# A hybrid encoder layer on one core: attention steps handed out ahead of the norm and rotation pieces

## The chip, the core and the metric

The kernel runs on one core of a Trainium2 chip, in one launch. The metric is the device time in microseconds. Five engines work side by side, each through its own queue in program order: TensorE (PE in the profile, with its weight loads as PEld), VectorE (DVE), ScalarE (ACT), GpSimd (POOL) and SyncE (SP), which issues most transfers. An instruction that waits holds everything behind it on its own engine.

## The reference

One layer over 512 tokens of width 1024, in float32. Three token mixers run in parallel, are gated and merged, and an expert-choice mixture of experts follows:

```python
z = x @ w_in                       # NA q|k|v, GQA q|k|v, memory q, gates
y_na  = neighbourhood_attention(q_na, k_na, v_na, rpb)     # 8 heads of 64
# gqa_attention, 8 query heads and 2 key heads of 64:
q = apply_rope(rms_norm(q, q_gain), cos, sin)
k = apply_rope(rms_norm(k, k_gain), cos, sin)
y_gqa = softmax(q @ k.T / sqrt(64)) @ v
y_mem = softmax(q_m @ mk.T / sqrt(128)) @ mv               # 4 heads of 128, 256 memory tokens
merged = sum_g sigmoid(gate_g(x)) * (y_g @ w_branch[g])
x = LN(alpha * x + merged @ w_out)
x = LN(alpha * x + ExpertChoiceMoE(x))                     # 16 experts, SwiGLU, capacity 64
```

The change touches the part in which the rotated, normalised queries and keys of the second mixer (GQA) are made, and the order in which the attention of the first two mixers to run (memory, then GQA) is handed out beside it.

## The kernel before, in words

The order of work on every engine is written out by hand: the program text is the order. A dense product is kept exact enough by splitting both factors into a high and a low part and adding three products; the weights stream in as 74 units of 128 x 1024 (`Stream`, transfers issued on SyncE, split on ScalarE (high, L87) and VectorE (low, L88)).

The stages are generators. Each `yield` in one of them ends a *round*: the products of this round have been issued on TensorE, and their evacuation from PSUM follows when the generator goes on. `run(gen, every, delay)` walks through the rounds and puts two sorts of work into each:

- a *piece* from the list `bg`, at most one for each round;
- an *attention step* (`at.step`), when the count `acc`, which grows by `every` in each round, has reached 1.

A step advances a pipeline over three attention units at once: the scores S of a new unit, the transposes T of the unit before, the product PV of the one before that, all on TensorE; then `soft` (maximum on VectorE, exponential on ScalarE), `tev` (evacuation of the transposes), `norm` (scaling by the reciprocal sum on VectorE, L536) and `yev`. T of a unit, one step later, reads what `norm` wrote. The scores have two PSUM banks (tag "S"), the transposes two ("T"), PV one ("Y"), and all dense products and the rotation transposes share three ("mm").

The pieces of GQA's rotary part come from `rope_stages`, one list for each group of heads: group 0 is the keys, groups 1 and 2 are four query heads each. A list is: s1 the square (ACT, L360); s2 the sum of squares and a reciprocal root in small VectorE instructions (L363 to L96); s3 two multiplications (VectorE, L368, L369); s4 the rotation, six instructions on POOL (L379 to L382); then transposes on TensorE with copies on ScalarE and subtractions on VectorE: `sk` for the keys (rT at L388, kk at L396 and L398), `sq_(0)` and `sq_(1)` for the two head pairs of a query group (rT at L388, qs at L408 and L409). Below, a0 to a5 are the six pieces of group 1 and b0 to b5 those of group 2, counted as in the diff (a[4] is a4); so a3 and b3 are the rotations, and a4, a5, b4, b5 the transposes. All groups share one scratch for squares and rotation.

`g_gqa` has twelve rounds, four for each group ("projection rounds" 1 to 12), each of 24 products of 256 columns. Its memory-attention steps come at `every` = 0.85. A group's list is added to `bg` behind its fourth round. Then `g_branch(2)` runs ("branch rounds" 1 to 16): two gate products of 24 matmuls of 512 columns each, then two projections of 12, four times over. GQA's steps begin in branch round 4 and come in every round. After it follow the value rounds of the neighbourhood attention (`g_na_v`) with the rest of the steps.

Before the change the pieces fall on these rounds: keys s1 to s4 on projection rounds 5 to 8, `sk` on 9; a0 to a2 on 10 to 12; a3 on branch round 1, a4 on 2, a5 on 3; b0 to b5 on 4 to 9; then `norm_hi`, `norm_mask` and `norm_lo`, which prepare rows of the layer norms, on 10 to 12. In each round the piece stands ahead of the step.

Later stages use `run` too: `g_na_gates` has a short list of router pieces beside steps of the neighbourhood attention. The expert stage at the end streams its weights through a ring of lent buffers: when TensorE has used up the block in a buffer, the transfer of the next block into it is issued.

Of the kernel before, what the change touches and what calls it, by code (L numbers as in the profile page):

```python
# [59 lines left out]
def layer_kernel(ctx: ExitStack, tc: tile.TileContext, xt, xn, first0, wu, bgate, rpb, gains, wrt,  # L60
# [14 lines left out]
    def R(tag, shape, name, dt=F32, bufs=None):  # L75
        return rp.tile(shape, dt, name=name, tag=tag, bufs=bufs)
# [3 lines left out]
    def PB(tag, name, shape=(P, 512)):  # L80
        return ps.tile(list(shape), F32, name=name, tag=tag, bufs=PS_BUFS[tag])

    def small(shape, name, dt=F32, bufs=2):
        return sp.tile(shape, dt, name=name, tag=name, bufs=bufs)
# [5 lines left out]
    def rsqrt(y, v, hv, a):  # L90
        nc.vector.tensor_scalar(y.bitcast(I32), v.bitcast(I32), -0.5, RSQRT_SEED, op0=ALU.mult, op1=ALU.add)
        nc.vector.tensor_scalar(hv, v, -0.5, None, op0=ALU.mult)
        for _ in range(3):
            nc.vector.tensor_tensor(a, y, y, op=ALU.mult)
            nc.vector.tensor_tensor(a, a, hv, op=ALU.mult)
            nc.vector.scalar_tensor_tensor(y, a, 1.5, y, op0=ALU.add, op1=ALU.mult)  # L96
# [181 lines left out]
    def n_chunk(acc, us, ah, al, m, hooks={}):  # L278
        c = slice(m * P, (m + 1) * P)
        for k in range(KD):  # L280
            hooks.get(k, lambda: None)()
            h = us[k // 4][0].rearrange("p (k c) -> p k c", k=4)[:, k % 4]
            lo = us[k // 4][1].rearrange("p (k c) -> p k c", k=4)[:, k % 4]
            nc.tensor.matmul(acc, ah[:, k, c], h, start=(k == 0), stop=False)
            nc.tensor.matmul(acc, ah[:, k, c], lo, start=False, stop=False)
            nc.tensor.matmul(acc, al[:, k, c], h, start=False, stop=(k == KD - 1))
# [60 lines left out]
    bg = []  # L347

    def rope_stages(q, zs, nh, which):
        n = NT * nh  # L350
        z = zs.rearrange("p m (h f) -> p (m h) f", f=64)
        sqf, t = ST["rope"]
        sq = sqf[:, :n * 64].rearrange("p (g f) -> p g f", f=64)
        t = t[:, :n * 64]
        zr = ST["zr"][:, q % 2, :n * 64]
        ss = small([P, n], f"ss{n}", bufs=1)
        rs = small([P, n], f"rs{n}", bufs=1)

        def s1():
            nc.scalar.activation(sq, z, AF.Square)  # L360

        def s2():
            nc.vector.tensor_reduce(ss, sq, axis=AX.X, op=ALU.add)  # L363
            nc.vector.tensor_scalar(ss, ss, 1.0 / 64.0, RMS_EPS, op0=ALU.mult, op1=ALU.add)
            rsqrt(rs, ss, small([P, n], f"sh{n}", bufs=1), small([P, n], f"sa{n}", bufs=1))

        def s3():
            nc.vector.tensor_tensor(z, z, rs[:, :, None].to_broadcast([P, n, 64]), op=ALU.mult)  # L368
            nc.vector.tensor_tensor(z, z, gain_t[:, which, None, :].to_broadcast([P, n, 64]), op=ALU.mult)  # L369

        def s4():
            z2 = zs.rearrange("p m (h i two) -> p m h i two", i=32, two=2)
            u2 = sqf[:, :n * 64].rearrange("p (m h i two) -> p m h i two", m=NT, i=32, two=2)
            t2 = t.rearrange("p (m h i two) -> p m h i two", m=NT, i=32, two=2)
            d2 = zr.rearrange("p (m h i two) -> p m h i two", m=NT, i=32, two=2)
            cb = csn_t[:, :, 0, None, :].to_broadcast([P, NT, nh, 32])
            sb = csn_t[:, :, 1, None, :].to_broadcast([P, NT, nh, 32])
            for i in range(2):
                nc.gpsimd.tensor_tensor(t2[:, :, :, :, i], z2[:, :, :, :, i], cb, op=ALU.mult)  # L379
                nc.gpsimd.tensor_tensor(u2[:, :, :, :, i], z2[:, :, :, :, 1 - i], sb, op=ALU.mult)  # L380
            for i, op in enumerate((ALU.subtract, ALU.add)):
                nc.gpsimd.tensor_tensor(d2[:, :, :, :, i], t2[:, :, :, :, i], u2[:, :, :, :, i], op=op)  # L382

        def heads_T(pair):
            tp = PB("mm", f"rT{q}{pair}", (P, NT, P))
            zc = zr.rearrange("p (m c) -> p m c", m=NT)
            for m in range(NT):
                nc.tensor.transpose(tp[:, m], zc[:, m, pair * P:(pair + 1) * P], ident)  # L388
            return tp.rearrange("p m c -> p (m c)")

        def sk():
            tp = heads_T(0)
            for g in range(2):
                src = tp[g * 64:g * 64 + 64]
                for o in (0, 64):
                    nc.scalar.copy(khh[o:o + 64, g], src)  # L396
                for o in (0, 64):
                    nc.vector.tensor_tensor(klo[o:o + 64, g], src, khh[o:o + 64, g].bitcast(F32), op=ALU.subtract)  # L398

        def sq_(pair):  # L400
            hp = 2 * (q - 1) + pair
            tp = heads_T(pair)
            for h in range(2):
                src = tp[h * 64:h * 64 + 64]
                d = ST["qs"][hp // 2][:, 2 * (hp % 2) + h]
                hb = 64 * (hp // 2)
                lb = 64 - hb
                nc.scalar.copy(d[hb:hb + 64], src)  # L408
                nc.vector.tensor_tensor(d[lb:lb + 64], src, d[hb:hb + 64].bitcast(F32), op=ALU.subtract)  # L409

        khh, klo = ST["khh"], ST["klo"]
        if which:
            return [s1, s2, s3, s4, sk]
        return [s1, s2, s3, s4, lambda: sq_(0), lambda: sq_(1)]

    def g_gqa():
        kk = R("Q6", [P, 4, S], "kk", F32R)
        qs = R("Q4", [P, 8, S], "qs", F32R)
        ST["b01"] = b01 = R("Q5", [P, 4, 1024], "ropevg")
        b1t = b01[:, 2:4]  # L420
        vg = b1t[:, 0, :512].rearrange("p (m f) -> p m f", m=NT)
        ST.update(khh=kk[:, 0:2], klo=kk[:, 2:4], vg=vg, qs=(qs[:, 0:4], qs[:, 4:8]),
                  rope=(vs_t[:, 0], b1t[:, 1]), zr=b01[:, 0:2])
        for q in range(3):
            us = ws.take(2)
            zs = ST["A5" if q % 2 else "A6"][:, 1, :512 if q == 0 else 1024].rearrange("p (m c) -> p m c", m=NT)
            for m in range(NT):
                acc = PB("mm", f"gq{q}{m}")
                n_chunk(acc[:, :256], us, xh, xl, m)
                ws.prefetch(2 if m == NT - 1 else 1)  # L430
                yield
                if q == 0:
                    nc.scalar.copy(zs[:, m], acc[:, :P])
                    nc.scalar.copy(vg[:, m], acc[:, P:256])
                else:
                    nc.scalar.copy(zs[:, m], acc[:, :256])
            bg.extend(rope_stages(q, zs, 2 if q == 0 else 4, 1 if q == 0 else 0))

    def g_na_v():
        v = ST["b01"][:, 0:2].rearrange("p a (b f) -> p (a b) f", f=S)  # L440
# [28 lines left out]
    def g_branch(g, first, pre=None):  # L469
        if first:  # L470
            ST["macc"] = R("M", [P, KD, S], "macc")
        macc = ST["macc"]
        for jp in range(4):
            th = []
            for jj in range(2):
                t = R("t", [P, S], f"th{g}{jp}{jj}", bufs=2)
                th.append(t)
                ev = gate_piece(g, 2 * jp + jj, t)
                yield
                ev()  # L480
            u, = ws.take()
            ws.prefetch()
            for jj in range(2):
                j = 2 * jp + jj
                acc = proj_piece(u, jj, *ST[f"y{g}"], f"pr{g}{j}")
                yield
                if first:
                    nc.vector.scalar_tensor_tensor(macc[:, j], th[jj], 1.0, acc, op0=ALU.add, op1=ALU.mult)
                else:
                    tmp = R("tmp", [P, S], f"tm{g}{j}", bufs=2)  # L490
                    nc.vector.scalar_tensor_tensor(tmp, th[jj], 1.0, acc, op0=ALU.add, op1=ALU.mult)
                    nc.gpsimd.tensor_tensor(macc[:, j], macc[:, j], tmp, op=ALU.add)
            if pre:
                yield from pre(jp)
# [265 lines left out]
    def run(gen, every=0.0, delay=0):  # L760
        acc = -every * delay
        for _ in gen:
            if bg:
                bg.pop(0)()
            acc += every
            while acc >= 1.0:
                acc -= 1.0
                at.step()


    class Ring:
# [84 lines left out]
    yg = R("Q2", [P, 8, S], "yg", F32R)  # L856
    ST["y1"] = (yg[:, 0:4], yg[:, 4:8])
    at.add([GqaUnit(hp, m) for hp in range(4) for m in range(NT)])
    bg.extend([norm_hi, norm_mask, norm_lo])
    run(g_branch(2, True), 1.0, 3)  # L860
    run(g_na_v(), 1.0)
    at.drain()
# [866 lines left out]
```

## Time and profile before

| | |
|---|---|
| runs | 977.21, 979.08, 1060.49 us; median 979.08 |
| profiled execution | 977.92 us |
| its span in the profile | 976.1 us |
| granted TensorE clock, mean | 0.995 |
| TensorE busy | 944.4 us, 97% of the span |
| VectorE, ScalarE, GpSimd busy | 451.9, 274.3, 78.4 us |
| moved by DMA | 251.62 MB, 258 GB/s in the mean |

Busy time counts instructions of an engine, not its queue's waits. The span is measured from the first to the last instruction that the profile shows, and 1.8 us of the profiled execution lie outside it. The stage that the change touches runs from about 80 to 180 us. In the views used below, a row of the order of time is: start, length, engine, line, operation, output<-inputs, shape, count, and in brackets the idle time before it and what released it. A row of waits is: who waited for whom, us in total, times, the longest. Line numbers are those of the kernel before.

### The profile page before, as it was taken

Reading aid. Unit: us, or ns where it says so; the run is one execution under the profiler, and the core shown is the slowest. Engines: PE = TensorE matmul, PEld = TensorE weight load, DVE = VectorE, ACT = ScalarE, POOL = GpSimd, SP = SyncE. Lnnn points to the kernel's source line nnn. Section 1 sums busy time; section 2 is a strip of 40 time slices with the busy share of each in tenths; the row PEclk is TensorE's granted clock in tenths of the full one; section 3 lists DMA queues with packets and bytes.
Section 4 is the critical chain, followed back from the end, with each engine's and each line's share of the span. In section 5 each row is a group of like instructions: output and inputs, shape, how many; then the busy total and the mean of one; then the engine's idle time right before and its main releaser. Section 6 shows DMA issues by size and latency. Waiting matters only on the chain.

```text
span 976.1 us, 13068 instructions
## 1 busy us (share of the span) xinstructions
PE 944.4 (97%) x5350; PEld 615.0 (63%) x5350; DVE 451.9 (46%) x857; ACT 274.3 (28%) x540; POOL 78.4 (8%) x86
## 2 busy tenths in 40 slices
PE   8999899999999999999999999999999998997996
PEld 8899787889888888887886333433343332432344
DVE  6347678765376566237464155331332222231426
ACT  5343345444354454323223000100010000100123
POOL 0002403000032231000013000000000000000003
PEclk9999999999999999999999999999999999999998
DMA  9312121111333322584719999999999999999992
GB/s 357 111 68 65 65 65 44 65 44 58 85 117 111 101 82 75 217 325 183 279 50 389 389 422 430 430 433 429 429 430 430 430 430 431 432 429 431 428 419 100
DMA packets 38473, 251.62 MB, mean 258 GB/s; under 512 B 12543, under 2 KB 12927, under 8 KB 24590
## 3 DMA queue, kind: packets, MB, share of 16 engines
q1 hardware_dynamic: 37982, 249.74, 63.5%
q10 hardware_dynamic: 432, 1.05, 0.3%
q8 instruction: 42, 0.69, 0.3%
q14 instruction: 17, 0.14, 0.0%
HBM read 247.89 MB, written 2.10 MB: 256 GB/s over the span
## 4 chain that ended last, share of the span: by engine, by line
PE 70%; DMA 18%; DVE 6%; ACT 2%; POOL 2%; issue 1%; SPq 0%; DVEq 0%; POOLq 0%; ACTq 0%
DMA w<-in_wx 17%; PE g L1254 7%; PE u L1254 7%; PE y L1287 6%; PE gate L269 4%; PE gate L271 4%; PE gate L270 4%; PE nqk L271 1%; PE nqk L270 1%; PE nqk L269 1%; PE gy L627 1%; PE pr L269 1%; PE pr L270 1%; PE pr L271 1%; PE ga L1216 1%
## 5 line engine op out<-in xcount | busy, mean ns | idle before, releaser
L1254 PE MATMUL g<-w,xs 128*64 128x512 f32 x512 | 134.7, 604 | 7.5 <-DMA w<-in_wx 7.5
L1254 PE MATMUL u<-w,xs 128*64 128x512 f32 x512 | 131.6, 592 | 0.0
L1287 PE MATMUL y<-w,hT 128*64 128x512 f32 x480 | 107.0, 594 | 4.6 <-DMA w<-in_wx 3.9
L87 ACT CAST y<-y 64x512 fp32r<-64x512 f32 x30 | 17.4, 579 | 240.3 <-PE y L1287 229.0
L88 DVE TENSOR_TENSOR y<-y,y 64x512 fp32r<-64x512 f32 x30 | 20.7, 689 | 135.2 <-ACT y L87 135.2
L1254 PEld LDWEIGHTS u<-w,xs 128*64 128x64 f32 x512 | 36.8, 137 | 73.1 <-issue 71.7
L1287 PEld LDWEIGHTS y<-w,hT 128*64 128x64 f32 x480 | 33.7, 137 | 74.4 <-issue 63.4
L88 DVE TENSOR_TENSOR los<-raw_twin,whi 128x1024 fp32r<-128x1024 f32 x43 | 54.0, 1257 | 51.3 <-ACT whi L87 51.0
L271 PE MATMUL gate<-xh,los 128*128 128x512 f32 x192 | 74.8, 390 | 0.0
L1254 PEld LDWEIGHTS g<-w,xs 128*64 128x64 f32 x512 | 31.3, 136 | 63.7 <-issue 48.0
L269 PE MATMUL gate<-xh,whi 128*128 128x512 f32 x160 | 63.6, 398 | 0.0
L270 PE MATMUL gate<-xl,whi 128*128 128x512 f32 x160 | 62.4, 390 | 0.0
L1357 DVE TENSOR_TENSOR acc<-acc,cb 128x512 f32<-128x512 f32 x56 | 35.4, 683 | 34.5 <-PE cb L1355 34.5
L87 ACT CAST whi<-raw_twin 128x1024 fp32r<-128x1024 f32 x43 | 45.2, 1051 | 7.3 <-PE wo L1062 4.4
L88 DVE TENSOR_TENSOR los<-raw_twin,los 128x1024 fp32r<-128x1024 f32 x21 | 27.4, 1305 | 36.6 <-ACT los L87 36.5
L1426 POOL TENSOR_TENSOR acc<-acc,ln2g 128x512 f32<-128x512 f32 x6 | 7.6, 1279 | 435.4 <-issue 433.4
L271 PEld LDWEIGHTS gate<-xh,los 128*128 128x128 f32 x192 | 36.1, 188 | 7.7
L603 ACT ACTIVATE att_twin<-gs,nm 128x512 f32<-128x512 f32 x32 | 21.7, 683 | 51.4 <-DVE nm L602 51.4
L1264 ACT ACTIVATE tg<-g 128x512 f32<-128x512 f32 x16 | 9.6, 597 | 94.0 <-PE g L1254 94.0
L1275 DVE COPY hT<-ht 128x512 f32<-128x512 f32 x15 | 10.4, 690 | 54.6 <-PE ht L1272 54.6
L269 PEld LDWEIGHTS gate<-xh,whi 128*128 128x128 f32 x160 | 30.0, 188 | 7.5 <-issue 1.0
L270 PEld LDWEIGHTS gate<-xl,whi 128*128 128x128 f32 x160 | 30.1, 188 | 5.9
(405 smaller groups left out, 1883.9 us busy)
## 6 DMA issues: line engine op xcount, KB each, us to landing
w<-in_wx SPq DMA_DIRECT2D x86, 2048.0 KB
raw_twin<-in_wu SPq DMA_DIRECT2D x65, 512.0 KB
w<-in_wx SPq DMA_DIRECT2D x20, 1024.0 KB
raw<-in_wu SPq DMA_DIRECT2D x8, 512.0 KB
xr<-in_xt SPq DMA_DIRECT2D x4, 512.0 KB
macc<-in_xn SPq DMA_DIRECT2D x2, 1024.0 KB
first<-in_first SPq DMA_DIRECT2D x4, 384.0 KB
bf<-in_rpb SPq DMA_DIRECT2D x64, 24.0 KB
```

Source lines behind the costliest of these rows:

```text
L87: nc.scalar.copy(hi, src)
L88: nc.vector.tensor_tensor(lo, src, hi.bitcast(F32), op=ALU.subtract)
L269: nc.tensor.matmul(acc, w_h, rh[:, k], start=(k == 0), stop=False)
L270: nc.tensor.matmul(acc, w_h, rl[:, k], start=False, stop=False)
L271: nc.tensor.matmul(acc, w_l, rh[:, k], start=False, stop=(k == nk - 1))
L603: nc.scalar.activation(self.p[:, h], self.s[h], AF.Exp, bias=nm[:, h:h + 1], accum_out=self.sm[:, h:h + 1])
L627: nc.tensor.matmul(self.y[h * 64:h * 64 + 64, :P], ST["vg"][:, kc, kvh * 64:kvh * 64 + 64], self.pt[:, h, kc], start=(kc == 0), stop=(kc = ...
L1216: nc.tensor.matmul(g, XH[:, m, c], oh[:, m], start=(m == 0), stop=False)
L1254: nc.tensor.matmul(GU[e][b][hf * 64:hf * 64 + 64], xs, w[b][:, hf * 512:hf * 512 + 512], start=(k == 0), stop=(k == KD - 1))
L1275: nc.vector.tensor_copy(t, tp)
L1287: nc.tensor.matmul(y[o * 64:o * 64 + 64], hT[:, c, hf * 64:hf * 64 + 64], w[j][:, o * 512:(o + 1) * 512], start=(k == 0 and j == 0), stop= ...
L1357: nc.vector.tensor_tensor(a, a, cb, op=ALU.add)
```

## The change

It does two things. `run` hands out the attention step of a round first and the piece after it, in all stages. And `g_gqa` no longer adds whole lists: of group 1 only the first four pieces are added behind its rounds, and the rest of groups 1 and 2 is written out as one list behind the third group's rounds, with an empty place ahead of a4, b0 between a4 and a5, and `norm_hi` between b3 and b4.

```diff
+        rope = []
         for q in range(3):
...
-            bg.extend(rope_stages(q, zs, 2 if q == 0 else 4, 1 if q == 0 else 0))
+            rope.append(rope_stages(q, zs, 2 if q == 0 else 4, 1 if q == 0 else 0))
+            bg.extend(rope[q] if q == 0 else rope[q][:4] if q == 1 else [])
+        a, b = rope[1:]
+        bg.extend([lambda: None, a[4], b[0], a[5], b[1], b[2], b[3], norm_hi, b[4], b[5]])
...
     def run(gen, every=0.0, delay=0):
         acc = -every * delay
         for _ in gen:
-            if bg:
-                bg.pop(0)()
             acc += every
             while acc >= 1.0:
                 acc -= 1.0
                 at.step()
+            if bg:
+                bg.pop(0)()
...
-    bg.extend([norm_hi, norm_mask, norm_lo])
+    bg.extend([norm_mask, norm_lo])
```

With it the pieces fall on these rounds: keys and a0 to a3 as before; the empty place on branch round 2, a4 on 3, b0 on 4, a5 on 5, b1 to b3 on 6 to 8, `norm_hi` on 9, b4 on 10, b5 on 11, `norm_mask` on 12, `norm_lo` on 13. No instruction is added or taken away on any engine; the transfers are issued in the same order.

## Prediction

> **What bounds the kernel now.** I read the page first, then busy time by stage, then TensorE's waits, then the order of time around each wait. The page says that TensorE is busy nearly throughout:
>
> ```profile
> PE 944.4 (97%) x5350; PEld 615.0 (63%) x5350; DVE 451.9 (46%) x857; ACT 274.3 (28%) x540; POOL 78.4 (8%) x86
> ```
>
> The stage table (width, then busy PE, PEld, DVE, ACT, POOL with counts, granted clock, DMA share, GB/s) says where it is not:
>
> ```profile
> 80.00:98.93 18.93, 17.12 (x136) 16.36 (x135) 12.59 (x24) 9.39 (x26) 5.46 (x6) 1.00 0.18 56
> 114.00:121.26 7.26, 5.58 (x26) 4.30 (x24) 1.29 (x1) 1.63 (x2) 7.20 (x5) 1.00 0.44 144
> 146.00:156.00 10.00, 8.60 (x54) 6.39 (x53) 9.17 (x15) 5.75 (x15) 9.20 (x6) 1.00 0.18 55
> 156.00:240.00 84.00, 84.00 (x613) 70.91 (x612) 56.16 (x107) 40.60 (x96) 0.00 (x0) 1.00 0.14 47
> 240.00:420.00 180.00, 180.00 (x996) 151.66 (x995) 97.47 (x155) 76.18 (x152) 32.38 (x36) 1.00 0.37 121
> 490.00:500.00 10.00, 10.00 (x61) 8.61 (x60) 5.03 (x23) 1.51 (x6) 0.73 (x3) 1.00 0.00 0
> 860.00:946.00 86.00, 78.19 (x353) 26.96 (x350) 23.05 (x38) 10.67 (x18) 0.00 (x0) 1.00 1.01 430
> ```
>
> The change works between 80 and 180 us. TensorE is idle there for 18.93 - 17.12 = 1.81 us, 7.26 - 5.58 = 1.68 us and 10.00 - 8.60 = 1.40 us: 4.89 us, 0.5% of the span, which is the most that any reordering here can return. From 156 to 420 us it is never idle. The waits between 60 and 240 us put the same 4.9 us down to two causes, a late rotation and a late normalisation:
>
> ```profile
> PE rT L388 <- POOL ropevg L382: 2.1, 2, 1.7
> PE mt L563 <- DVE att_twin L536: 1.8, 1, 1.8
> PE gt L614 <- DVE att_twin L536: 1.0, 2, 0.8
> ```
>
> Whether time saved here reaches the end: the expert stage is bound by its weight stream (DMA share 1.01 at 430 GB/s in 860 to 946 us), but at 490 to 500 us the queue moves nothing at 0 GB/s: every buffer lent to it is full, and it starts again when TensorE has used one. So the stream is released by TensorE, and mixers that end earlier move it earlier by as much. I take the passage as whole.
>
> **The change, part by part.** No instruction is added or removed, and SP's order of transfers stays as it is. What moves: in every round with a piece waiting, the attention step (S, T, PV, softmax, evacuations) now stands ahead of the piece on PE, DVE, ACT and POOL. Rotation transposes a4, a5 go from branch rounds 2 and 3 to 3 and 5; the norm pieces b1, b2, b3 of the third group from 5, 6, 7 to 6, 7, 8; b4, b5 from 8 and 9 to 10 and 11. b0 stays in round 4. The copy of the norm rows moves from round 10 to 9; it is one ACT copy with no reader there.
>
> *The first wait (98.93 us).* The key piece of the ninth projection round runs ahead of that round's softmax:
>
> ```profile
> 90.59 0.60 PE L388 MATMUL rT<-ident,ropevg 128*128 128x128 f32 x4
> 92.43 1.38 DVE L398 TENSOR_TENSOR kk<-rT,kk 64x512 fp32r<-64x512 f32 x2 [1.14 <-ACT kk L396]
> 95.05 1.40 DVE L398 TENSOR_TENSOR kk<-rT,kk 64x512 fp32r<-64x512 f32 x2 [1.24 <-ACT kk L396]
> 96.09 1.03 PE L545 MATMUL ms<-mkvzs,qmT 128*128 128x256 f32 x4
> 96.48 0.69 DVE L552 TENSOR_REDUCE nm<-ms 128x2 f32<-128x512 f32 x1
> 98.43 0.39 ACT L436 COPY mkvzs<-gq 128x256 f32<-128x256 f32 x1
> 98.52 0.62 DVE L536 TENSOR_SCALAR att_twin<-att_twin,rc 128x256 f32<-128x256 f32 x2
> 98.93 0.70 PE L563 MATMUL mt<-ident,att_twin 128*128 128x128 f32 x4 [1.81 <-DVE att_twin L536]
> 100.44 0.36 PE L284 MATMUL gq<-whi,xh 128*128 128x256 f32 x1
> ```
>
> The maximum at 96.48 had its scores, which TensorE makes right behind the rT of 90.59, since about 92 us and waited for VectorE to finish L398 (95.05 + 1.40). From maximum to normalised weights takes 98.52 + 0.62 - 96.48 = 2.66 us. Ahead of the piece this chain would run from about 91.6 to 94.3 us, well before the transposes of round 10 (about 96.5). Gain 1.81 us. What is late instead: the key piece runs from its transpose (now some 92.3) for as long as before, 96.45 - 90.59 = 5.86 us, its ACT copies ending near 97.3, and the evacuation of the round's product, queued behind them on ACT, ends near 97.7. That product's PSUM buffer is wanted by the second product after it, which would start at 100.44 - 1.81 - 0.4 = 98.2. A margin of 0.5 us; I charge nothing and keep 1 us of loss as the bound.
>
> *The second wait (121.26 us).* The rotation of the first query group is handed out one round before its transposes:
>
> ```profile
> 108.58 1.22 DVE L368 TENSOR_TENSOR mkvzs<-mkvzs,rs 128x1024 f32<-128x1024 f32 x1
> 108.69 0.37 ACT L87 CAST ym<-my 128x256 fp32r<-128x256 f32 x1 [1.29 <-PE my L574]
> 111.22 1.30 POOL L379 TENSOR_TENSOR ropevg<-mkvzs,consts 128x512 f32<-128x512 f32 x1 [22.16 <-DVE mkvzs L369]
> 118.25 2.95 POOL L382 TENSOR_TENSOR ropevg<-ropevg,ropesq 128x512 f32<-128x512 f32 x2
> 119.19 0.39 PE L271 MATMUL gate<-xh,los 128*128 128x512 f32 x1
> 121.26 0.66 PE L388 MATMUL rT<-ident,ropevg 128*128 128x128 f32 x4 [1.68 <-POOL ropevg L382]
> ```
>
> Now a projection of 12 matmuls stands between: 147.55 - 144.69 = 2.86 us by the rows further down. The transposes come at about 119.43 + 2.86 = 122.3, while POOL ends at 121.2, plus about 0.9 because the step now goes first and L368 has to wait for the memory output (copied on ACT at 108.69, subtracted after) instead of starting at 108.58: 122.1. Both move together with the first gain. The wait goes, with a margin of 0.2 us; I charge 0.2, bounds 0 and 0.9.
>
> *The third place (148 to 155 us).* Here three pieces of the third group overtake the softmax:
>
> ```profile
> 134.39 1.21 DVE L363 TENSOR_REDUCE ss<-ropesq 128x16 f32<-128x1024 f32 x1
> 137.73 0.17 DVE L96 SCALAR_TENSOR_TENSOR rs<-sa,rs 128x16 f32<-128x16 f32 x1
> 141.79 0.39 PE L593 MATMUL gs<-kk,qs 128*128 128x512 f32 x1
> 144.42 1.22 DVE L369 TENSOR_TENSOR mkvzs<-mkvzs,consts 128x1024 f32<-128x1024 f32 x1
> 144.69 0.50 PE L269 MATMUL pr<-ym,los 128*128 128x512 f32 x1
> 145.56 1.28 DVE L602 TENSOR_REDUCE nm<-gs 128x1 f32<-128x512 f32 x2
> 147.02 0.68 ACT L603 ACTIVATE att_twin<-gs,nm 128x512 f32<-128x512 f32 x1
> 147.55 0.39 PE L593 MATMUL gs<-kk,qs 128*128 128x512 f32 x1
> 148.02 2.10 DVE L536 TENSOR_SCALAR att_twin<-att_twin,rc 128x512 f32<-128x512 f32 x2
> 150.24 2.11 DVE L88 TENSOR_TENSOR los<-raw_twin,whi 128x1024 fp32r<-128x1024 f32 x1
> 150.26 0.63 PE L614 MATMUL gt<-ident,att_twin 128*128 128x128 f32 x4 [0.81 <-DVE att_twin L536]
> 155.25 0.66 PE L388 MATMUL rT<-ident,ropevg 128*128 128x128 f32 x4 [0.39 <-POOL ropevg L382]
> ```
>
> The scores of round 6 were written from 141.79 us on, their maximum began only at 145.56, behind L368 and L369; the weights were normalised at 150.12, and the transposes of round 7 waited 1.0 us. Then b4's transposes waited 0.39 us for a rotation begun one round earlier.
>
> After: the round-6 maximum starts where L368 did, 144.42 - 1.22 = 143.20. From there to normalised weights I take 148.02 - 145.56 + 2 x 0.63 = 3.72 us (0.63 is the mean in the groups below), so 146.9, ahead of the transposes, which follow the four score products (an estimate: 12 products take 2.86 us, so four take 0.9) at 147.55 + 0.9 = 148.45. That wait goes. What is late next is the round-7 maximum: behind it now stand b1 (137.73 + 0.17 - 134.39 = 3.51 us) and the weight split (1.38), so it starts at 146.9 + 4.9 = 151.8 instead of 148.5 and the first half is normalised at 151.8 + 3.72 - 0.63 = 154.9. The transposes of round 8 are due after a step (144.69 - 141.79 = 2.90) and a projection (2.86) from 147.55, plus 0.9: 154.2. I charge 0.7 us of new wait, bounds 0 and 1.4. b4 comes two rounds after b3, so the 0.39 us goes.
>
> A rotation on POOL also slows VectorE:
>
> ```profile
> L536 DVE TENSOR_SCALAR att_twin<-att_twin,rc 128x512 f32<-128x512 f32 x10 | 5.9, 631 | 0.2
> L88 DVE TENSOR_TENSOR los<-raw_twin,whi 128x1024 fp32r<-128x1024 f32 x6 | 8.3, 1384 | 5.1 <-ACT whi L87 5.1
> ```
>
> The pair of L536 at 148.02 took 2.10 us against 2 x 0.63 = 1.26 us in the mean, the split 2.11 against 1.38; the maxima (1.28) took no longer. The change moves this into rounds 8 and 9, of which 9 holds a gate product of twice the matmuls; I charge nothing, bounds 0 and 1.2. The Trainium skill's page "SBUF — State Buffer", section "Who interferes with whom", says that VectorE and GpSimd share a port pair as an exclusive lock, held for a whole instruction, and that a tensor_reduce on trn2 does not take it. The rows agree; by that rule the lock follows b3 wherever it is put, and its result is the second case below.
>
> *The sum.* 1.81 + 1.68 + 1.0 + 0.39 = 4.9 us removed; 0.2 + 0.7 charged; 4.0 us gained. The profiled execution took 977.92 us, 1.82 more than its span of 976.1; less 4.0 that is 973.9, say 974.0. The median of the runs shown, 979.08, stands 1.2 above the profiled one, and the fastest, 977.21, stands 0.7 below; the same gain from these gives 975.1 and 973.2.
>
> **The rivals.** *The wait moves with the rotation.* POOL's rotation now meets the normalisation of rounds 8 and 9 and the split between them: 0.84 + 0.73 us by the rows above, and the transposes wait again. For it: the transposes at 150.26 us waited under exactly this pair. Against: a gate round is longer. Gain 4.0 - 1.6 = 2.4 us: 975.5.
>
> *Slower: VectorE's backlog reaches the score banks.* The scores have two PSUM banks, and each step fills both, so S of one round waits until the exponentials of the round before have read them. With b1, the split and b2 (2 x 1.22 = 2.44 us) between the softmaxes, S itself is held in rounds 8 and 9, and TensorE with all that is queued behind it: 3.51 + 2.44 = 5.95 us, all exposed, against 4.9 removed, gives 977.92 + 1.05 = 979.0. The second exponential ends 147.02 + 0.68 - 145.56 = 2.14 us after the maximum begins, and the second bank is wanted at about 147.55 + 2.90 + 2.86 + 0.45 = 153.8, so it decides from a maximum that begins after 151.6. I find 151.8: the point is reached, by 0.2 us. Against: only the excess costs, and the backlog of b2 falls into round 9, whose product is twice as long.
>
> *No change.* The order of pieces moves, but the end does not, because the weight stream sets it: 977.9. For it, the 430 GB/s; against it, the 10 us without any transfer before.
>
> **How the numbers follow.** Forecast 0.60 (own range 972.5 to 975.4), moved wait 0.20, slower 0.12, no change 0.08. The range runs from 971.0 (all 4.9 us off the fastest run, and a little more) to 979.5, past the slower case. Two per cent, some 19.6 us, is about what a measurement of this kernel can tell from no change. With only 4.9 us to win, over 2% faster is all but excluded (0.01); over 2% slower needs a wait in many rounds that I do not see (0.03); 0.96 within.
>
> **What would show it.** In the changed profile: no wait of mt on L536 near 97 us; rT's waits on L382 summing under 0.5 us; gt's on L536 under 1 us; POOL's last rotation starting about a round later, past 150 us; TensorE idle by under 1.5 us between 80 and 180; the weight stream starting about 4 us earlier. I am wrong if gs waits for ACT, if a gq product waits for the copies of kk, if gt's waits exceed 2 us, or if TensorE's saving in the mixers is there and the span has not shrunk.

## The result, and the profile after

The changed kernel takes 974.44 us (median of 6, 973.67 to 974.95); before, measured with it, 978.71 (median of 6). One of those six, the 1060.49 us of the table above, was in a slower state of the chip; the ratio leaves it out. The ratio is 0.9955, 95% interval [0.9944, 0.9966]: some 4.4 us less. The change is small but clear of the noise, and the interval of 0.0011 to either side is far finer than the two per cent that the prediction took as the limit of what can be told. Forecast were 974.0 us and a range of 971.0 to 979.5.

The page of the changed kernel (its span is 973.1 us, the execution 974.95), and busy time in 80 to 180 us, of the kernel before and then of the changed one:

```profile
PE 943.4 (97%) x5350; PEld 614.9 (63%) x5350; DVE 453.1 (47%) x857; ACT 274.8 (28%) x540; POOL 81.1 (8%) x86
```

```profile
80.00:180.00 100.00, 95.08 (x597) 80.58 (x596) 72.08 (x133) 46.56 (x101) 24.82 (x18) 1.00 0.18 59
```

```profile
80.00:180.00 100.00, 97.71 (x625) 83.93 (x624) 75.76 (x147) 46.80 (x102) 25.73 (x18) 1.00 0.19 64
```

TensorE is idle for 2.29 us there instead of 4.92. The waits of TensorE between 60 and 240 us after the change say what is left:

```profile
PE rT L388 <- POOL ropevg L382: 1.8, 1, 1.8
PE mt L567 <- DVE att_twin L540: 0.3, 1, 0.3
```

All of gt's 1.0 us and 1.5 of mt's 1.8 us are gone, and so is b4's 0.39 us. But the longest of rT's waits, the one that the spacing was to remove, is as long as it was (1.68 before, 1.81 now). So two of the signs that the prediction named did not come: rT's waits under 0.5 us, and TensorE idle by under 1.5 us.

A better ruler than the span, which holds the weight stream too, is the stretch from the start of the first scores of the memory attention to the start of the last group of products of the GQA attention (order of time, before and then after):

```profile
59.50 1.03 PE L545 MATMUL ms<-mkvzs,qmT 128*128 128x256 f32 x4
...
242.00 1.09 PE L627 MATMUL gy<-att_twin,ropevg 128*64 128x128 f32 x16
```

```profile
58.91 1.03 PE L549 MATMUL ms<-mkvzs,qmT 128*128 128x256 f32 x4
...
237.78 1.09 PE L631 MATMUL gy<-att_twin,ropevg 128*64 128x128 f32 x16
```

182.50 us became 178.87: 3.63 us less. The length of this stretch, the *mixer stretch*, is used for all runs below; in three executions whose program is the changed one up to the end of this stretch it is 178.85, 178.87 and 178.89.

### The profile page after: what moved, and what is told of

The parts are those of the page before. It is cut to its first block, busy times and chain, and to the rows that moved or that the text cites. A ratio compares the mean times of both kernels' runs of the same rounds, so it can differ in the third digit from the quotient of the medians.

```text
span 973.1 us, 13068 instructions
## 1 busy us (share of the span) xinstructions
PE 943.4 (97%) x5350; PEld 614.9 (63%) x5350; DVE 453.1 (47%) x857; ACT 274.8 (28%) x540; POOL 81.1 (8%) x86
## 4 chain that ended last, share of the span: by engine, by line
PE 72%; DMA 17%; DVE 6%; ACT 1%; issue 1%; POOL 1%; SPq 0%; DVEq 0%; POOLq 0%; ACTq 0%
DMA w<-in_wx 17%; PE g L1258 8%; PE u L1258 7%; PE y L1291 6%; PE gate L269 4%; PE gate L271 4%; PE gate L270 4%; PE pr L269 2%; PE gy L631 2%; PE pr L270 2%; PE pr L271 2%; PE nqk L271 1%; PE nqk L270 1%; PE nqk L269 1%; PE gt L618 1%
## 5 line engine op out<-in xcount | busy, mean ns | idle before, releaser
L88 DVE TENSOR_TENSOR y<-y,y 64x512 fp32r<-64x512 f32 x30 | 20.7, 689 | 135.6 <-ACT y L87 135.6
L88 DVE TENSOR_TENSOR los<-raw_twin,whi 128x1024 fp32r<-128x1024 f32 x43 | 54.2, 1260 | 51.3 <-ACT whi L87 51.1
L88 DVE TENSOR_TENSOR los<-raw_twin,los 128x1024 fp32r<-128x1024 f32 x21 | 26.6, 1268 | 35.0 <-ACT los L87 34.9
```

What stands on the lines that cost most here:

```text
L88: nc.vector.tensor_tensor(lo, src, hi.bitcast(F32), op=ALU.subtract)
```

## The experiments

| kernel | median us | ratio, 95% interval | mixer stretch us |
|---|---|---|---|
| changed | 974.44 | 0.9955 [0.9944, 0.9966] | 178.87 |
| order only | 979.72 | 1.0012 [1.0002, 1.0022] | 185.33 |
| list only | 979.18 | 1.0007 [0.9997, 1.0017] | 184.60 |
| early sums | 973.00 | 0.9943 [0.9928, 0.9958] | 177.66 |
| changed, again | 973.76 | 0.9953 [0.9938, 0.9968] | 178.89 |
| keys later | 970.99 | 0.9925 [0.9908, 0.9942] | 175.76 |
| delay | 1019.46 | 1.0423 [1.0407, 1.0439] | 178.85 |
| order only, wait filled | 979.26 | 1.0011 [1.0002, 1.0021] | 183.15 |

**Order only.** The kernel before with

```diff
-            if bg:
-                bg.pop(0)()
             acc += every
             while acc >= 1.0:
...
+            if bg:
+                bg.pop(0)()
```

> Only the new order inside a round (step first); the pieces stay on their old rounds. Theory A (the two parts do different work: the order frees the softmaxes, the spacing frees the transposes from POOL): the first wait goes (mt on VectorE 0.3 us instead of 1.8), but a4's transposes stand in branch round 2 and POOL still ends as late as after the whole change, so rT waits some 4.8 us there and about 1 us at b4; TensorE's waits from 60 to 240 us sum to about 6 us, time 978 to 981 us, ratio 1.000 to 1.003. Rival B (the order alone carries the gain, the spacing adds little): waits under 3 us, ratio 0.996 to 0.997.

Its waits of TensorE from 60 to 240 us:

```profile
PE rT L388 <- POOL ropevg L382: 4.6, 2, 3.5
PE gt L614 <- DVE att_twin L536: 0.8, 1, 0.8
PE mt L563 <- DVE att_twin L536: 0.3, 1, 0.3
```

5.7 us, close to theory A's sum of about 6: mt waits only 0.3 us, and the transposes, on their old rounds, wait for POOL twice as long as before (3.5 us; 4.8 were expected). The order alone gains nothing; rival B falls. The stretch is 2.84 us longer, which is more than the waits say; the last experiment returns to this.

**List only.** The changed kernel with the old order inside `run`.

> Only the new list of pieces; within a round the piece goes first, as before. Theory A: the first wait stays at 1.8 us, POOL ends at about 121 us as before and a4's transposes come after it, so rT waits 0 to 0.3 us; b1 and b2 stand ahead of the softmaxes of rounds 6 and 7, so gt waits 1 to 2 us; sum 3 to 4 us, ratio 0.998 to 0.999. Rival B (the list alone carries the gain): sum under 2.5 us, ratio 0.996. Rival C (rT's wait of 1.8 us after the change comes from POOL and VectorE slowing each other and not from the later start): rT still waits over 1 us here.

```profile
PE mt L567 <- DVE att_twin L540: 1.8, 1, 1.8
PE gs L597 <- ACT att_twin L607: 1.4, 1, 1.4
PE gt L618 <- DVE att_twin L540: 1.0, 2, 0.8
```

4.2 us. rT does not wait: with the old order the same spacing is enough. That does not settle rival C, for POOL was not slowed here. Its six instructions take 119.30 + 3.02 - 112.27 = 10.05 us, against 9.98 before and 10.85 after the change:

```profile
112.27 1.30 POOL L379 TENSOR_TENSOR ropevg<-mkvzs,consts 128x512 f32<-128x512 f32 x1 [23.68 <-DVE mkvzs L369]
...
119.30 3.02 POOL L382 TENSOR_TENSOR ropevg<-ropevg,ropesq 128x512 f32<-128x512 f32 x2
```

mt's 1.8 us is back. New is a wait of the scores (gs) for the exponentials of the round before: b1 and b2 ahead of the softmax push it back until the two score banks are held. That is the mechanism of the prediction's slower case; the order takes it away. The time was a miss: a ratio of 0.998 to 0.999 was expected, and 1.0007 came. So neither half gains, and both together take some 4.4 us off.

**Early sums.** The changed kernel, with a1 and a2 ahead of their rounds' steps:

```diff
+        s2.early = s3.early = q == 1
...
         for _ in gen:
+            early = bool(bg) and getattr(bg[0], "early", False)
+            if early:
+                bg.pop(0)()
             acc += every
...
-            if bg:
+            if bg and not early:
                 bg.pop(0)()
```

> The changed kernel, but the sum of squares and the multiplications of the first query group (a1, a2) go ahead of their rounds' steps. Theory A (the changed kernel's rT still waits 1.8 us because a1 queues on VectorE behind the step of projection round 11, so that POOL starts no earlier though TensorE does): POOL's rotation of that group starts about 1.8 us earlier (near 109.7 instead of 111.5) and rT waits 0 to 0.4 us; ratio to before 0.9935 to 0.9945, some 1.5 us better than the changed kernel. Rival C (the instructions on POOL are slower, 10.85 us instead of 9.95 us for the six, because VectorE works beside them): POOL starts earlier, but takes 11 us or more, rT still waits over 1 us. Rival D: T in round 11 waits longer than 0.3 us behind a1, which gives the gain back.

**The changed kernel again**, measured beside early sums:

> The changed kernel once more, as the base for the three others: ratio 0.9944 to 0.9966 as measured; waits of TensorE from 60 to 240 us sum to 2.1 us, 1.8 of it rT on POOL.

It came out so. POOL's first and last rotation instruction of the first query group and the transposes that wait for them, first in the changed kernel (again), then with early sums:

```profile
111.22 2.14 POOL L379 TENSOR_TENSOR ropevg<-mkvzs,consts 128x512 f32<-128x512 f32 x1 [20.73 <-DVE mkvzs L369]
...
118.10 3.95 POOL L382 TENSOR_TENSOR ropevg<-ropevg,ropesq 128x512 f32<-128x512 f32 x2
122.10 0.66 PE L388 MATMUL rT<-ident,ropevg 128*128 128x128 f32 x4 [1.79 <-POOL ropevg L382]
```

```profile
110.07 1.30 POOL L379 TENSOR_TENSOR ropevg<-mkvzs,consts 128x512 f32<-128x512 f32 x1 [19.41 <-DVE mkvzs L369]
...
117.12 3.01 POOL L382 TENSOR_TENSOR ropevg<-ropevg,ropesq 128x512 f32<-128x512 f32 x2
121.08 0.60 PE L388 MATMUL rT<-ident,ropevg 128*128 128x128 f32 x4
```

POOL starts 1.15 us earlier (1.8 were expected) and takes 10.06 us instead of 10.83; the wait of 1.79 us is gone. So A holds and is the larger part. The other 0.77 us is a slowdown such as C named; that it comes from VectorE working beside POOL is argued, since no run varies it alone. What is left there (mt 0.3, and 0.5 us of my behind a late evacuation on VectorE) is rival D, in small: 1.23 us of the stretch are gained, the medians (973.00 and 973.76) differ the same way, but their intervals overlap.

**Keys later.** If VectorE's place in the queue decides when POOL starts, the group can be moved up by a whole round and the keys' transposes put behind it, into branch round 1, where no step stands:

```diff
-            bg.extend(rope[q] if q == 0 else rope[q][:4] if q == 1 else [])
-        a, b = rope[1:]
-        bg.extend([lambda: None, a[4], b[0], a[5], b[1], b[2], b[3], norm_hi, b[4], b[5]])
+            bg.extend(rope[q][:4] if q < 2 else [])
+        k, a, b = rope
+        bg.extend([k[4], lambda: None, a[4], b[0], a[5], b[1], b[2], b[3], norm_hi, b[4], b[5]])
```

> The changed kernel, but the first query group's first four pieces come one round earlier (projection rounds 9 to 12 hold a0 to a3) and the keys' transposes move behind them to branch round 1, where no attention step stands. Theory A: VectorE is free for a1 and a2 a round earlier, so POOL starts some 3 us or more earlier than 111.5 and rT waits 0 us at a4; the key piece no longer stands between two softmaxes, so mt's 0.3 us goes too; TensorE's waits from 60 to 240 us sum to under 0.5 us, ratio to before 0.993 to 0.9945, 1.5 to 2.5 us better than the changed kernel. Rival: the key transposes in branch round 1 hold the gate's PSUM bank or wait themselves, and 1 to 2 us come back.

POOL's first instruction, the transposes that it serves, and the busy time in 80 to 180 us:

```profile
106.24 2.13 POOL L379 TENSOR_TENSOR ropevg<-mkvzs,consts 128x512 f32<-128x512 f32 x1 [15.18 <-DVE mkvzs L369]
...
119.64 0.60 PE L388 MATMUL rT<-ident,ropevg 128*128 128x128 f32 x4
```

```profile
80.00:180.00 100.00, 100.00 (x647) 86.56 (x647) 77.81 (x152) 47.92 (x104) 24.77 (x18) 1.00 0.19 64
```

POOL starts 5 us earlier, TensorE has no wait left in the stretch, and the time is 970.99 us, ratio 0.9925 [0.9908, 0.9942]: the fastest version of this study, 3.1 us less in the mixer stretch than the changed kernel. That is better than the expected 0.993 to 0.9945. The rival did not show.

**Delay.** The changed kernel with a block of products ahead of the neighbourhood attention, where TensorE never waits:

```diff
     at.drain()
+    stall = PB("mm", "stall")
+    for _ in range(200):
+        nc.tensor.matmul(stall[:, :P], ident, ident, start=True, stop=True)
     na_bias(0)
```

> The changed kernel with 200 extra 128x128 products on TensorE, written to a bank that nothing reads, between the GQA stage and the neighbourhood attention, where TensorE never waits: 200 x 0.12 us = 24 us at the spacing of the products of that shape elsewhere. If time in the mixers passes to the end whole (theory A), the span grows by as much as the stall block itself takes, 23 to 25 us, ratio near 1.020. If the weight stream sets the end by itself (rival: no change), the span grows by far less, under 12 us.

The block in the trace (count; minimum, median and longest duration in ns; first and last start):

```profile
L869 PE MATMUL stall<-ident x400: 271/276/276, 247.5 to 292.0; 128*128 128x128 f32 x134
```

Each float32 product is issued twice, x400 for 200, so the block takes 44.8 us and not the 24 us expected: a miss in size. The time grows by 1019.46 - 974.44 = 45.0 us. What the mixers lose passes to the end whole; the no-change case falls. That what they gain passes too, a delay cannot show; "keys later" does, whose stretch is 6.74 us shorter than before and whose time is 977.94 - 970.99 = 6.95 us shorter than that of the kernel before measured with it. The weight stream moves along: its first transfer after the silent stretch starts at 506.9 us before, 502.7 after the change and 499.7 with keys later. A single execution can stray by a microsecond or two: the profiled ones of the kernel before and of keys later differ in span by 976.1 - 971.0 = 5.1 us only.

**Order only, with the wait filled.** Looking for why "order only" and "list only" were slower than their waits explain (5.7 and 4.2 us against 4.9 before, but 2.8 and 2.1 us more in the stretch), I found the granted clock (the third figure from the end of a row) of "order only" around its wait ("list only" has a shorter dip, shown in the last section):

```profile
116.00:120.00 4.00, 2.73 (x13) 1.92 (x11) 0.87 (x1) 0.00 (x0) 4.00 (x3) 1.00 0.41 138
120.00:124.00 4.00, 1.76 (x6) 1.58 (x7) 0.00 (x0) 0.58 (x1) 2.19 (x2) 0.63 0.00 0
124.00:128.00 4.00, 4.00 (x11) 3.12 (x10) 2.39 (x3) 2.20 (x3) 0.00 (x0) 0.52 0.00 0
520.00:528.00 8.00, 6.75 (x77) 5.60 (x76) 5.04 (x20) 2.93 (x6) 4.64 (x5) 1.00 1.02 431
```

So, in "order only", ahead of the first transposes:

```diff
+            if (q, pair) == (1, 0):
+                for _ in range(16):
+                    nc.tensor.matmul(tp[:, 0], ident, ident, start=True, stop=True)
```

> The new order alone (as in the run of the order only), with 16 extra products of 128x128 on TensorE (some 1.9 us) ahead of a4's transposes, in the time in which it waits for POOL. Theory E (the wait of 3.5 us costs twice: itself, and then 6.8 us at half the granted clock, 120.8 to 127.6 us in that run, because TensorE was idle too long): TensorE does useless work in the wait, the granted clock stays at 1.00 in 115 to 130 us, and the time falls by 2 to 3 us to about 977, though work was added. Rival F (the dip of the clock comes at random, not from the wait): the dip comes or not, and the median stays at 979 to 980 or rises.

```profile
118.00:122.00 4.00, 4.00 (x35) 3.81 (x34) 0.00 (x0) 0.00 (x0) 3.87 (x3) 1.00 0.29 112
122.00:126.00 4.00, 4.00 (x21) 3.18 (x22) 1.38 (x2) 2.61 (x4) 0.00 (x0) 1.00 0.00 0
...
520.00:524.00 4.00, 3.06 (x44) 2.67 (x44) 1.77 (x9) 0.70 (x3) 2.15 (x2) 0.86 1.02 430
524.00:528.00 4.00, 4.00 (x28) 3.17 (x27) 1.52 (x4) 0.56 (x1) 0.00 (x0) 0.71 1.00 424
```

The products, 3.73 us of them, fill the wait; the clock stays at 1.00 there, and the stretch is 2.18 us shorter although work was added. But in this execution the clock falls at 520 to 528 us, where "order only" had 1.00, and the median hardly moves (979.26 against 979.72, ratios 1.0011 and 1.0012). The kernel before has a dip at that place too (0.50 from about 522.5 to 525.9 us), so the filling need not have brought it. The mean granted clock over the whole span is on record for each of the ten runs of both kernels: it averages 0.9941 in "order only" and 0.9957 with the wait filled, against 0.9959 and 0.9954 in the runs of the kernel before that were measured with them. So the loss of clock in "order only" is no accident of one execution. Theory E holds for the clock and fails for the time, which stays where F put it; why the time does not follow is open.

## Why the prediction was right, and where its steps were not

*The passage: right; the ceiling: wrong.* The delay and "keys later" show that time lost or saved in the mixers reaches the end. But the 4.89 us of idle time are not the most that any reordering can return: "keys later" returned 6.74 us of the stretch and 6.95 us of the time.

*The first wait: right but for a third of a microsecond.* The softmax ahead of the key piece freed 1.5 of 1.81 us; the rest came back as a wait of 0.34 us one round later, since the next maximum (at 99.02 us) now queues behind the key piece (L398 until 98.98). The margin of 0.5 us on the PSUM bank held.

*The second wait: wrong.* The step that failed is "Both move together with the first gain". TensorE did move: it finished the projection at 120.24 + 0.39 = 120.63, near the 122.3 - 1.81 = 120.5 worked out. POOL did not: by the prediction it would end at 122.1 - 1.81 = 120.3, and it ended at 122.39. The sum of squares, then the rotation with the ends of the gate product and the projection beside it, and the transposes after the change:

```profile
103.66 0.42 DVE L88 TENSOR_TENSOR ym<-my,ym 128x256 fp32r<-128x256 f32 x1 [0.76 <-ACT ym L87]
104.00 1.21 DVE L363 TENSOR_REDUCE ss<-ropesq 128x16 f32<-128x1024 f32 x1
...
111.54 2.15 POOL L379 TENSOR_TENSOR ropevg<-mkvzs,consts 128x512 f32<-128x512 f32 x1 [20.73 <-DVE mkvzs L369]
...
117.52 0.39 PE L271 MATMUL gate<-xh,los 128*128 128x512 f32 x1
...
118.42 3.97 POOL L382 TENSOR_TENSOR ropevg<-ropevg,ropesq 128x512 f32<-128x512 f32 x2
...
120.24 0.39 PE L271 MATMUL pr<-ym,los 128*128 128x512 f32 x1
122.44 0.66 PE L388 MATMUL rT<-ident,ropevg 128*128 128x128 f32 x4 [1.81 <-POOL ropevg L382]
```

and the sum of squares before:

```profile
102.22 1.21 DVE L363 TENSOR_REDUCE ss<-ropesq 128x16 f32<-128x1024 f32 x1
```

The prediction looked at L368 only and missed a1, one round earlier: it now stands behind the step of projection round 11 on VectorE, whose last instruction (L88 at 103.66) waits for ACT and so for TensorE's PV. L363 starts 1.8 us later, while TensorE is 119.19 - 117.52 = 1.7 us ahead at the end of the gate product. Of the 2.1 us by which POOL ended too late, 1.2 are its start (111.54 instead of 111.22 + 0.9 - 1.81 = 110.3) and 0.9 its six instructions, which took 10.85 us instead of 9.98; the prediction let POOL slow VectorE, but not the other way round. 0.2 us was charged, 0.9 at most; 1.81 us was the price. "Early sums" shows the late start as a cause by removing it; the slowdown went with it, and its own cause stays argued.

*The third place: right in kind, 0.7 us charged for nothing.* Round 7's scores, maximum, normalisation, round 8's transposes, and the normalisation beside b3's rotation:

```profile
145.53 0.39 PE L597 MATMUL gs<-kk,qs 128*128 128x512 f32 x1
148.42 1.28 DVE L606 TENSOR_REDUCE nm<-gs 128x1 f32<-128x512 f32 x2
150.88 0.88 DVE L540 TENSOR_SCALAR att_twin<-att_twin,rc 128x512 f32<-128x512 f32 x2
152.23 1.03 PE L618 MATMUL gt<-ident,att_twin 128*128 128x128 f32 x8
157.32 2.79 DVE L540 TENSOR_SCALAR att_twin<-att_twin,rc 128x512 f32<-128x512 f32 x2
```

The maximum begins 2.9 us after its scores (4.25 were worked out) and the weights are ready at 151.76, 0.5 us ahead of the transposes. The durations taken were means that held instructions slowed by POOL: 0.63 each for L536 where the undisturbed pair takes 0.88 in all.

*The rivals.* The rotation did meet the normalisation (2.79 us at 157.32, the slowest of all), but in a round with room: no wait. The wait of the slower case, gs for ACT, came only with the old order (list only).

*The sum.* Waits of 4.9 us fell to 2.1, about 2.7 us less and not 4.0: the second wait took 1.6 us more than was charged for it and the first gave 0.3 us less, while the 0.7 us charged in the third place never came. Yet the stretch shrank by 3.63 us, 0.9 more than the waits. A wait costs more than the idle time that the view shows: with all 4.9 us gone ("keys later") the stretch is 6.74 us shorter than before, though the granted clock is 1.00 throughout the stretch in both. Part of it can be read from the rows. Twelve projection products take 2.86 us, so one starts 0.24 us behind the other, but each is shown some 0.39 us long; ahead of a wait the last one is counted busy to its end, 0.15 us more. For five waits that makes, by estimate, 0.8 of the 1.8 us; the rest is open. So the number was met by luck: 1.9 us overlooked in two waits stood against 0.7 us charged for nothing and 0.9 us that the idle time does not show. What the time gained beyond the 3.63 us lies outside the stretch, where two executions of one program differ by more than that.

## What to carry to other kernels

When a piece of work is moved behind another in a hand-written order, every instruction of its chain has to be followed back on every in-order queue: here the spacing helped only with the order, the order only with the spacing, and the order itself delayed the start of the chain whose end it was to cover. Put the head of a long chain (small sums on one engine, a rotation on another) into a round in which its engine is free, ahead of spacing out its end. To know whether a stage sets the end, delay it by a known amount and see whether the end follows; whether a gain reaches the end needs a run that gains. And do not take the idle time of a view as the most that can be won.

## What the runs showed of the hardware

A short wait of TensorE can go with a halved clock behind it. In "order only" the granted clock was 0.50 from some 121.0 to 127.9 us, worked out from the rows at 120 and 124 us (0.37 and 0.48 of 4 us lost, at half a clock 6.8 us in all); it fell while TensorE still stood in its wait of 3.5 us, which ended at 122.2. In the changed kernel's routing stage, with shorter gaps, two rows of 4 us show 0.81 and 0.77, which is 0.50 for 3.4 us; in "changed, again", the same program, it stayed at 1.00 there (stages of the changed kernel, then of the same again):

```profile
516.00:520.00 4.00, 3.62 (x47) 3.19 (x48) 2.11 (x8) 0.49 (x2) 1.37 (x2) 0.81 1.00 430
520.00:524.00 4.00, 4.00 (x27) 2.65 (x27) 1.23 (x3) 0.56 (x1) 0.00 (x0) 0.77 1.02 424
```

```profile
508.00:528.00 20.00, 18.49 (x162) 13.50 (x161) 9.44 (x36) 7.51 (x11) 7.77 (x9) 1.00 0.96 409
```

Whether a given wait brings it differs from one execution to the next. The two executions of the changed program differ by 2.1 us in span (973.1 and 971.0) with equal mixer stretches, but only 0.8 us of it arises at this dip, between 517 and 525 us; some 1.0 us arises in the expert stage, where the clock is 1.00 in both. The Trainium skill's page "TensorE: Matmul & The Clock Gate", Part 1, describes a clock at half rate after an idle window of about 3.4 us that runs freely; the value 0.50, the lengths of 3.4 and 6.8 us and the varying place agree. It does not agree that a whole window of idling is needed: in "list only" the clock fell about a microsecond behind mt's wait of 1.8 us. In the kernel before, the same wait at the same place left it at 1.00 (list only, then before):

```profile
96.00:100.00 4.00, 2.19 (x13) 1.56 (x13) 3.41 (x8) 2.89 (x9) 0.00 (x0) 0.94 0.00 0
100.00:104.00 4.00, 4.00 (x25) 4.00 (x24) 3.33 (x12) 1.29 (x6) 0.00 (x0) 0.63 0.00 0
```

```profile
96.00:100.00 4.00, 2.19 (x15) 1.54 (x14) 3.38 (x9) 2.51 (x7) 0.00 (x0) 1.00 0.00 0
100.00:104.00 4.00, 4.00 (x37) 4.00 (x36) 3.41 (x11) 1.55 (x6) 0.00 (x0) 1.00 0.00 0
```

Little of the 4.4 us can come from fewer such dips. The profiled executions of the kernel before and of the changed one have, apart from the last microseconds of the span, one dip each, both of 3.4 us in the routing stage, and none in the mixer stretch, where the 3.63 us arose. Over all runs the mean granted clock is 0.9959 (20 runs of the kernel before) and 0.9960 (five of "changed, again", measured beside them), though single runs scatter by 0.002.
